# A norm turned by VectorE and DRAM instead of TensorE, in a two-layer decoder trunk

## The chip, the cores and the metric

The kernel runs on one core of one Trainium2 chip. The metric is the device time of one execution in microseconds; for the kernel before it is the median of three runs, 1269.65 us (1269.5 to 1270.11).

A core has a matrix engine (TensorE; PE in the profile, its weight loads PEld), VectorE (DVE), ScalarE (ACT) and GpSimd (POOL), and a fifth engine, SyncE (SP), that only issues transfers. Each engine works through its own queue in order. TensorE accumulates into banks of PSUM, from which VectorE and ScalarE read.

## What is computed

Two layers over 256 tokens of width 1024, all in float32. Cut to what matters here, one layer is

```python
h = layer_norm(ALPHA * x + 0.5 * swiglu(x, ffn1_w_gu, ffn1_w_down), ln_g[0], ln_b[0])
(dn_q, dn_k, dn_v, dn_b, dn_a, dn_z, sw_q, sw_k, sw_v, xa_q, gates) = split(h @ w_in)
o_dn = deltanet_branch(...)              # gated delta rule
o_sw = sliding_window_attention(...)     # banded attention
o_xa = memory_cross_attention(xa_q, mem_n, w_mem_kv)   # k, v = split(mem_n @ w_mem_kv)
merged = sum over branches of sigmoid(gates) * (branch @ w_branch)
h = layer_norm(ALPHA * h + merged @ w_out, ln_g[1], ln_b[1])
x = layer_norm(ALPHA * h + 0.5 * swiglu(h, ffn2_w_gu, ffn2_w_down), ln_g[2], ln_b[2])
```

The change concerns the first of the three norms of each layer, the one that stands ahead of the three mixers, and the matmuls that come next.

## The kernel before, in words

**Tiling.** The 256 tokens are two blocks of 128 rows (`tb` 0 and 1). A matmul contracts over 128 partitions, so the activations are also needed with features on partitions: `hT`, eight slices of 128 features by 256 tokens. The matmuls take operands of the format fp32r, so every operand is split into a high part (a rounded copy, made by ScalarE) and a low part (the rest, made by VectorE): `split`, line 125. Each product is three matmuls, high by high, high by low, low by high (`mm3`, line 139).

**Weights** come in one stream, in units of at most 128 x 1024 (`unit`, line 104). SyncE loads a unit into one of four `raw` buffers, ScalarE and VectorE split it into one of five `whi` and five `wlo` buffers. Units are scheduled ahead of other work, and each buffer comes free when TensorE has used it.

**Order.** The program is traced once, and a planner orders each engine's queue by priority and by its own model of times. The kernel bends this order in two ways. `tc.issue_after(x)` puts instructions behind `x` in the queue of `x`'s engine. `pinned` keeps TensorE's instructions in program order; it is on in the mixers.

**Around the norm.** The down projection of the feed-forward (`Ffn.rest`, line 375, which calls `projA`, line 181) ends with the last four units for the first block, then for the second. `Post` (line 395) adds the residual and normalises: `layernorm` (line 268) takes the statistics, then multiplies twice (lines 291 and 296), in two halves of 512 columns. After each half `fin(c)` calls `to_T` (line 249): four TensorE transposes of 128 x 128 through PSUM (line 137, tile `sm`), then a split from PSUM into `hT`. For the first block these calls are kept back as `turns`, and `projA` runs them between the last matmul groups of the second block; for the second block they are made at once.

**Behind the norm** come the memory projections (`memory_kv`, line 512), which don't need `hT`: keys with four units (96 matmuls of width 256), values with four units (48 of width 512). The low halves of the value units stand behind the norm's last instruction on VectorE (`behind=post.end`, `held`). The values are copied out of PSUM by ScalarE (line 521). Then the mixers begin with the first projection of `h`, 648 columns wide (line 529): eight units, each used for six matmuls of width 324 by each block. The last three units (`tail`) are kept and used block after block; the first five go unit by unit, both blocks each. The four PSUM banks of this projection are those that the memory keys and values held before.

**The DRAM trip** that the change uses is in the kernel already, in the feed-forward (`Ffn.out`, lines 353 to 363, and `settle`): VectorE's transpose turns each 32 x 32 block on its own (line 356), GpSimd issues four writes to a DRAM tile `tr` (line 362) and one read back as `pt` (line 363), which puts the 32 x 32 blocks where they belong. ScalarE and VectorE then split `pt`.

On GpSimd's queue two memsets (lines 849 and 850) prepare buffers for the delta rule's inverses.

Of the kernel before, what the change touches and what calls it, by code (L numbers as in the profile page):

```python
# [17 lines left out]
P = 128  # L18
D = 1024
S = 256  # L20
# [3 lines left out]
KD = D // P  # L24
# [4 lines left out]
MOD = 648  # L29
# [9 lines left out]
def tile_trunk(ctx, tc, x, xT, mem, memT_, wst, lnp, memln, cvw, rows, cst, out):  # L39
    nc = tc.nc  # L40
# [83 lines left out]
    def split(hi, lo, src):  # L124
        return nc.scalar.copy(hi, src).ins, nc.vector.tensor_tensor(lo, src, hi.bitcast(F32), op=ALU.subtract).ins  # L125
# [183 lines left out]
    class Ffn:  # L309
        def __init__(self, before=None):  # L310
            self.units = []
            for q in range(KD // 2):
                if before:
                    before(q)
                self.units.append(unit(cuts=2 if before and q == 0 else 1, parts=2 if before and q in (1, 2) else 1))
            self.hu, self.bank, self.due = {}, {}, []
# [77 lines left out]

    class Post:

        def __init__(self, g_ap, b_ap, last=False):
            self.aps, self.last, self.hT = (g_ap, b_ap), last, None

        def early(self, bank):  # L400

# [6 lines left out]
        def __call__(self, tb, outs):  # L408
            if tb == 0:
                self.gb = gb(*self.aps)  # L410
                self.hT = None if self.last else new_hT()
            y = hres[tb]

            def put(q):
                return self.hT[0][:, q * 4:q * 4 + 4, :], self.hT[1][:, q * 4:q * 4 + 4, :]

            def src(j, c):
                nc.vector.scalar_tensor_tensor(y[:, c], outs[tb][j], 0.5 / ALPHA, y[:, c], op0=ALU.mult, op1=ALU.add)

            turns = []  # L420

            def fin(c):
                if self.last:

                    cc = slice(c * 512, (c + 1) * 512) if not tb else slice(*((0, 512), (512, 768), (768, 1024))[c])
                    (nc.scalar if c == 2 else nc.sync).dma_start(out[tb * P:(tb + 1) * P, cc], y[:, cc])
                elif tb == 0:

                    turns.append(lambda: to_T(put, tb, y, c))
                else:  # L430
                    to_T(put, tb, y, c)

            self.end = layernorm(y, *self.gb, 1, src, fin, [o.shape[-1] for o in outs[tb]], (512, 256, 256) if self.last and tb else (512, 512))
            return turns

    def begin(nxt, hT):
# [72 lines left out]
            return {8: lambda: again(0), 12: lambda: once(0), 14: lambda: again(1), 18: lambda: once(1)}  # L509
        return {4: vecs, 6: lambda: sums(0), 8: rows_, 11: halves_, 12: lambda: quarter(0), 14: lambda: quarter(1), 16: lambda: quarter(2), 18: lambda: quarter(3)}  # L510

    def memory_kv(mT, behind):
        mx = (lambda k: mT[k // 4][:, k % 4, :], lambda k: mT[2 + k // 4][:, k % 4, :])
        mkT = (T(pu, [P, 4, S], "u10", F32R), T(pu, [P, 4, S], "u7", F32R))
        for i, b in enumerate(projB(mx, 4, 2)):
            split(*(t[:, 2 * i:2 * i + 2, :] for t in mkT), b)
        mv_ = T(pu, [P, 2, 512], "u11")
        outs = [[acc()] for _ in range(2)]
        projA(mx, 512, 2, KD, outs, behind=behind, held=range(4))
        for tb in range(2):  # L520
            nc.scalar.copy(mv_[:, tb, :], outs[tb][0])
        return mkT, mv_

    def mixers(l, hT, mkT, mv_, post):
        xt = acc_of(hT)
        pinned[0] = True

        outs = [[acc()[:, :MOD // 2] for _ in range(2)] for _ in range(2)]
        projA(xt, MOD, 1, KD, outs, 3)
        ba = T(pu, [P, 2, 8], "ba")  # L530
        zs = T(pu, [P, 2, 512], "u3")
        swv = T(pu, [P, 2, P], "swv")
# [288 lines left out]
        def inverses():  # L821

            cp = T(p2, [P, 2, 4, 16], "t2", bufs=4)
            for c in range(2):
                tmp = T(p2, [P, 4, P], "t2", bufs=4)
                nc.vector.tensor_tensor(tmp, AK[c][:, :, 0, :], over4(cs[:, C_NB:C_NB + P]), op=ALU.mult)
                nc.vector.tensor_reduce(cp[:, c], tmp.rearrange("p h (d i) -> p h i d", i=16), axis=AX.X, op=ALU.add)
            dr = T(pd, [P, P], "dr")
            nc.gpsimd.dma_start(dr, cp.rearrange("p c h i -> p (c h i)"))
            blocks = dr.rearrange("(d j) n -> d (j n)", j=16)  # L830
            for t in range(2):
                src = blocks[:, t * 1024:(t + 1) * 1024].unsqueeze(1).to_broadcast([8, 16, 1024])
                nc.gpsimd.dma_start(TM[t].rearrange("p a h c -> p (a h c)"), src)
            for c in range(2):
                for q in qd:
                    nc.gpsimd.tensor_tensor(L32[q, c], AK[c][q, :, 0, q], cs[q, C_LV:C_LV + 32].unsqueeze(1).to_broadcast([32, 4, 32]), op=ALU.mult)

            y16 = T(p2, [P, 8, 16], "t2", bufs=4)
            pr16 = T(p2, [P, 8, 15], "t2", bufs=4)
            i16 = cs[:, C_I16:C_I16 + 16].unsqueeze(1).to_broadcast([P, 8, 16])  # L840
            nc.gpsimd.tensor_copy(y16, i16)
            ab = [TM[c].rearrange("p a h (n i) -> p (a h) n i", i=16) for c in range(2)]
            for j in range(15):
                n = 15 - j
                nc.gpsimd.tensor_tensor(pr16[:, :, 0:n], ab[j // 8][:, j % 8, :, j + 1:16], y16[:, :, j:j + 1].to_broadcast([P, 8, n]), op=ALU.mult)
                nc.gpsimd.tensor_tensor(y16[:, :, j + 1:16], y16[:, :, j + 1:16], pr16[:, :, 0:n], op=ALU.add)
            nc.gpsimd.tensor_tensor(Y32.rearrange("p c h (d i) -> p (c h) d i", d=2), y16.unsqueeze(2).to_broadcast([P, 8, 2, 16]),
                                    cs[:, C_BD:C_BD + 32].rearrange("p (d i) -> p d i", d=2).unsqueeze(1).to_broadcast([P, 8, 2, 16]), op=ALU.mult)
            nc.gpsimd.memset(Y, 0.0)
            nc.gpsimd.memset(X64[qd[0], :, :, 32:64], 0.0)  # L850

        W = T(pu, [P, 1024], "w0")
        X64, X32, Y32 = (W[:, a:b].rearrange("p (c h i) -> p c h i", c=2, h=4) for a, b in ((0, 512), (512, 768), (768, 1024)))
# [277 lines left out]
    for l in range(NL):  # L1131
        mT = []
        mid = memory_T(mT, l)
        if l == 0:

            mid[2] = lambda: load(cs, cst)
            more = {4: lambda *a: xres(0), 6: lambda *a: xres(1), 8: lambda *a: small()}
        post = Post(lnp[l, 0, 0], lnp[l, 0, 1])
        f1.rest(hT, 4, [((pu, "u0"), (pu, "u1")), ((pu, "u2"), (pu, "u3"))], post, mid, ends, {} if l else more)
        kv = memory_kv(mT, post.end)  # L1140
        if l == 0:
            nc.scalar.activation(nea, rw[:, :, 8:12], AF.Exp)
            nc.vector.tensor_scalar(nea, nea, -1.0, None, ALU.mult)
        post2 = Post(lnp[l, 1, 0], lnp[l, 1, 1])
        mixers(l, post.hT, *kv, post2)
        f2 = Ffn()
        begin(f2, post2.hT)
        last = l == NL - 1
        post = Post(lnp[l, 2, 0], lnp[l, 2, 1], last)
        f2.rest(post2.hT, 6, [((pu, a), (pu, b)) for a, b in (("u0", "u1"), ("u2", "u3"), ("u4", "u5"), ("u6", "u13"))], post, behind=post2.end)  # L1150
        ends = post.end
        if not last:
            f1, hT = Ffn(), post.hT
            begin(f1, hT)
# [9 lines left out]
def _stream(i):  # L1164
    parts = []
    for l in range(NL):
        def ffn(gu, dn):
            for c in range(0, FF, S):
                parts.append(_kcols(np.concatenate([gu[:, c:c + S], gu[:, FF + c:FF + c + S]], 1), 2))

            parts.append(_kcols(dn.reshape(FF // S, 4, 2, 32, D).transpose(0, 2, 1, 3, 4).reshape(FF, D), 1))
        ffn(i["ffn1_w_gu"][l], i["ffn1_w_down"][l])
        mk = i["w_mem_kv"][l]
        parts.append(_kcols(mk[:, :512], 2))
        parts.append(_kcols(mk[:, 512:], 2))
        w = i["w_in"][l]
        parts.append(_kcols(np.concatenate([w[:, 1536:2056], w[:, 2696:2824]], 1), 1))
        for s in (512, 0, 1024, 2824):
            parts.extend(_kcols(w[:, c:c + 256], 4) for c in (s, s + 256))
        parts.append(_kcols(w[:, 2568:2696], 8))  # L1180
        sq = w[:, 2056:2568].reshape(D, 2, 4, 64).transpose(0, 2, 1, 3).reshape(D, 512)
        parts.extend(_kcols(sq[:, s:s + 256], 4) for s in (0, 256))
        wb = i["w_branch"][l]
        for n in (2, 1, 0):
            for j in range(2):
                c = 3336 + n * D + j * 512
                parts.append(_kcols(w[:, c:c + 512], 2))
            b = wb[n]
            if n == 1:
                b = b.reshape(2, 4, 64, D).transpose(1, 0, 2, 3).reshape(512, D)  # L1190
            parts.append(_kcols(b, 1))
        parts.append(_kcols(i["w_out"][l], 1))
        ffn(i["ffn2_w_gu"][l], i["ffn2_w_down"][l])
    return np.concatenate(parts)
# [47 lines left out]
```

## Time and profile before

| | before |
|---|---|
| median of three runs | 1269.65 us |
| profiled execution | 1269.55 us |
| its span | 1267.8 us |
| TensorE busy | 1257.0 us (99%) |
| VectorE busy | 870.5 us (69%) |
| ScalarE busy | 661.0 us (52%) |
| GpSimd busy | 221.7 us (17%) |
| granted TensorE clock | 0.999 |
| DRAM traffic | 263.56 MB, mean 208 GB/s |

The span is the time from the first to the last instruction of the program; the time of an execution has a little more around it. Lines such as L134 are lines of the kernel, and `acc<-whi,hT` names an output tile and its inputs. In a timeline, the columns are start and duration in us, engine, line, operation, tiles, shape and count; a bracket gives idle time before the first of them and what ended it. In the chain of waits, the columns are start, duration, and the piece of work. Matmuls overlap in the pipeline, so the cost of one is the distance between starts, not its duration.

### The profile page before, as it was taken

Reading aid. Unit: us, or ns where it says so; the run is one execution under the profiler, and the core shown is the slowest. Engines: PE = TensorE matmul, PEld = TensorE weight load, DVE = VectorE, ACT = ScalarE, POOL = GpSimd, SP = SyncE. Lnnn points to the kernel's source line nnn. Section 1 sums busy time; section 2 is a strip of 40 time slices with the busy share of each in tenths; the row PEclk is TensorE's granted clock in tenths of the full one; section 3 lists DMA queues with packets and bytes.
Section 4 is the critical chain, followed back from the end, with each engine's and each line's share of the span. In section 5 each row is a group of like instructions: output and inputs, shape, how many; then the busy total and the mean of one; then the engine's idle time right before and its main releaser. Section 6 shows DMA issues by size and latency. Waiting matters only on the chain.

```text
span 1267.8 us, 18770 instructions
## 1 busy us (share of the span) xinstructions
PE 1257.0 (99%) x6916; PEld 1070.2 (84%) x6916; DVE 870.5 (69%) x1284; ACT 661.0 (52%) x982; POOL 221.7 (17%) x395
## 2 busy tenths in 40 slices
PE   9999999999999999999999999999999999999997
PEld 6888889999878888888888888899988788888886
DVE  6678576886667776665666656759767588766565
ACT  6456544665664544454454554456656654454441
POOL 1232100002331102221012220000033401122100
PEclk9999999999999999999999999999999999999999
DMA  8988765665554738887668886566564456588862
GB/s 293 315 270 280 253 212 157 210 183 132 169 152 147 250 136 256 242 242 222 216 206 245 257 256 216 183 184 205 163 167 134 134 191 225 179 245 244 241 223 80
DMA packets 78795, 263.56 MB, mean 208 GB/s; under 512 B 12528, under 2 KB 13968, under 8 KB 78704
## 3 DMA queue, kind: packets, MB, share of 16 engines
q1 hardware_dynamic: 66320, 232.40, 57.2%
q0 software_dynamic: 12240, 29.84, 8.8%
q8 instruction: 54, 0.88, 0.3%
q14 instruction: 37, 0.30, 0.1%
q10 hardware_dynamic: 144, 0.13, 0.0%
HBM read 247.48 MB, written 14.85 MB: 207 GB/s over the span
## 4 chain that ended last, share of the span: by engine, by line
PE 99%; DMA 0%; DVE 0%; SPq 0%; ACT 0%; issue 0%; DVEq 0%
PE acc L134 87%; PE at L134 4%; PE sm L134 3%; PE sm L137 1%; PE acc L332 1%; PE acc L333 1%; PE acc L335 1%; PE at L137 1%; DMA raw<-in_wst_dram 0%; DVE h L291 0%; DVE h L296 0%; SPq L115 0%; SPq L78 0%; ACT whi L125 0%; DVE bnst L277 0%
## 5 line engine op out<-in xcount | busy, mean ns | idle before, releaser
L125 DVE TENSOR_TENSOR wlo<-raw,whi 128x1024 fp32r<-128x1024 f32 (+2 forms) x405 | 487.2, 1210 | 277.0 <-ACT whi L125 275.2
L125 ACT CAST whi<-raw 128x1024 fp32r<-128x1024 f32 (+2 forms) x405 | 413.5, 1029 | 397.4 <-PE acc L134 317.2
L134 PE MATMUL acc<-whi,hT 128*128 128x512 f32 (+1 forms) x1824 | 562.1, 386 | 0.8 <-ACT whi L125 0.8
L134 PEld LDWEIGHTS acc<-whi,hT 128*128 128x128 f32 x1824 | 340.0, 188 | 72.0 <-ACT whi L125 2.7
L134 PE MATMUL acc<-wlo,hT 128*128 128x512 f32 (+1 forms) x912 | 350.3, 384 | 0.0
L134 PE MATMUL acc<-whi,u 128*128 128x512 f32 x812 | 259.5, 392 | 0.0
L134 PEld LDWEIGHTS acc<-wlo,hT 128*128 128x128 f32 x912 | 171.3, 188 | 33.3 <-DVE wlo L125 1.3
L134 PEld LDWEIGHTS acc<-whi,u 128*128 128x128 f32 x812 | 152.3, 188 | 32.1 <-DVE u L125 0.5
L134 PE MATMUL acc<-wlo,u 128*128 128x512 f32 x406 | 158.2, 390 | 0.0
L362 POOL DMA_DIRECT2D tr<-t x176 | 96.3, 554 | 314.0 <-DVE t L356 307.4
L134 PE MATMUL acc<-hT,whi 128*128 128x256 f32 x672 | 121.8, 284 | 0.0
L134 PEld LDWEIGHTS acc<-hT,whi 128*128 128x128 f32 x672 | 104.7, 192 | 0.0
L134 PE MATMUL acc<-hT,wlo 128*128 128x256 f32 x336 | 95.1, 283 | 0.0
L134 PEld LDWEIGHTS acc<-wlo,u 128*128 128x128 f32 x406 | 76.3, 188 | 15.4
L134 PEld LDWEIGHTS acc<-hT,wlo 128*128 128x128 f32 x336 | 64.4, 192 | 0.0
L363 POOL DMA_DIRECT2D pt<-tr x44 | 25.1, 570 | 192.0 <-DMA tr<-t 146.7
L353 ACT ACTIVATE t<-acc 128x256 f32<-128x256 f32 x88 | 33.5, 381 | 37.6 <-PE acc L134 37.6
L134 PE MATMUL acc<-u,u 128*128 128x512 f32 x186 | 46.4, 394 | 0.0
L354 DVE TENSOR_TENSOR t<-t,acc 128x256 f32<-128x256 f32 x88 | 36.7, 417 | 8.1 <-ACT t L353 4.1
L134 PEld LDWEIGHTS acc<-u,u 128*128 128x128 f32 x186 | 34.6, 188 | 7.5
L125 DVE TENSOR_TENSOR u<-pt,u 128x512 fp32r<-128x512 f32 x44 | 28.9, 657 | 9.3 <-ACT u L125 9.3
L553 DVE SCALAR_TENSOR_TENSOR t<-acc,cw,t 128x255 f32<-128x255 f32 (+2 forms) x72 | 34.5, 479 | 1.1
(245 smaller groups left out, 1164.3 us busy)
## 6 DMA issues: line engine op xcount, KB each, us to landing
raw<-in_wst_dram SPq DMA_DIRECT2D x409, 512.0 KB, 4.3
tr<-t POOLq DMA_DIRECT2D x176, 64.0 KB, 3.7
pt<-tr POOLq DMA_DIRECT2D x44, 256.0 KB, 5.0
raw<-in_wst_dram SPq DMA_DIRECT2D x16, 324.0 KB, 3.0
gB<-in_lnp_dram SPq DMA_DIRECT2D x6, 512.0 KB, 5.9
bB<-in_lnp_dram SPq DMA_DIRECT2D x6, 512.0 KB, 6.2
w<-dr POOLq DMA_DIRECT2D x4, 512.0 KB, 10.4
t<-in_xT_dram SPq DMA_DIRECT2D x4, 256.0 KB, 5.6
```

The costliest lines, as they stand in the source:

```text
L125: return nc.scalar.copy(hi, src).ins, nc.vector.tensor_tensor(lo, src, hi.bitcast(F32), op=ALU.subtract).ins
L134: return pe(nc.tensor.matmul(*a, **k))
L137: return pe(nc.tensor.transpose(*a))
L332: nc.tensor.matmul(ps, hT[0][:, k, ts], hi[:, c], start=k == 0, stop=False)
L333: nc.tensor.matmul(ps, hT[0][:, k, ts], lo[:, c], start=False, stop=False)
L335: nc.tensor.matmul(ps, hT[1][:, k, ts], hi[:, c], start=False, stop=k == KD - 1)
L353: act = nc.scalar.activation(t[:, :, tb, :], g, AF.Silu).ins
L354: ins = nc.vector.tensor_tensor(t[:, :, tb, :], t[:, :, tb, :], u, op=ALU.mult).ins
L362: nc.gpsimd.dma_start(d[:, :, q].rearrange("b c x -> c b x"), z[32 * q:32 * q + 32].rearrange("c (b x) -> c b x", b=4))
L363: back = nc.gpsimd.dma_start(y, d.rearrange("b c q x -> (b c) (q x)")).ins
L553: nc.vector.scalar_tensor_tensor(yc[:, j, d:], b[:, j, :S - d], w[:, t:t + 1], yc[:, j, d:], op0=ALU.mult, op1=ALU.add)
```

## The change

For the norm ahead of the mixers alone (`bounce=True`), the transposes leave TensorE. As soon as a half of a block is normalised, VectorE transposes it in 32 x 32 blocks (`leave`). After the second half of a block GpSimd issues four writes of 128 KB to a DRAM tile `tn`. After the second block's last write it issues four reads of 256 KB, two for each block. Back in `pt`, features stand on partitions in another order than before, so the rows of `w_in` are reordered on the host to match. `land` splits what came back into `hT`.

Where the splits stand is written out by hand. The first block's come behind the splits of the memory keys on both engines. The second block's come behind the last copy of the memory values on ScalarE. The first projection takes its first four units for the first block alone, then the same four for the second (`lead=4`). `post.end`, behind which the low halves of the value units stand, is now the second block's last VectorE transpose. The two memsets stand behind the last read.

```diff
     class Post:
+        def leave(self, tb, y, c):
+            if not c:
+                self.z = T(p2, [P, D], "pp")
+            cc = slice(c * 512, (c + 1) * 512)
+            ins = nc.vector.transpose(self.z[:, cc], y[:, cc]).ins
+            if c:
+                d = T(pd, [4, 32, 4, S], "tn")
+                for q in range(4):
+                    out_ = nc.gpsimd.dma_start(d[:, :, q].rearrange("b c x -> c b x"), self.z[32 * q:32 * q + 32].rearrange("c (b x) -> c b x", b=4)).ins
+                self.backs[tb] = d
+            if tb and c:
+                with tc.issue_after(out_):
+                    for t, d in self.backs.items():
+                        back = self.backs[t] = T(p2, [P, 2, 512], "pt")
+                        for i in range(2):
+                            self.read = nc.gpsimd.dma_start(back[:, i].rearrange("p (q x) -> p q x", q=4), d[:, :, :, i * P:i * P + P].rearrange("b c q x -> (b c) q x")).ins
+            return ins
+
+        def land(self, tb, c):
+            ts = slice(tb * P, (tb + 1) * P)
+            hi, lo = (self.hT[n][:, c * 4:c * 4 + 4, ts].rearrange("p k (q s) -> p q k s", q=4) for n in range(2))
+            return split(hi, lo, self.backs[tb][:, c].rearrange("p (q k s) -> p q k s", q=4, k=4))
...
+                elif self.bounce:
+                    self.left = self.leave(tb, y, c)
                 elif tb == 0:
                     turns.append(lambda: to_T(put, tb, y, c))
...
+            if self.bounce:
+                self.end = self.left
             return turns
...
-    def memory_kv(mT, behind):
+    def memory_kv(mT, post):
+        behind = post.end
...
         for i, b in enumerate(projB(mx, 4, 2)):
-            split(*(t[:, 2 * i:2 * i + 2, :] for t in mkT), b)
+            ends = split(*(t[:, 2 * i:2 * i + 2, :] for t in mkT), b)
+        with tc.issue_after(ends[0]), tc.issue_after(ends[1]):
+            for c in range(2):
+                post.land(0, c)
...
         for tb in range(2):
-            nc.scalar.copy(mv_[:, tb, :], outs[tb][0])
+            copied = nc.scalar.copy(mv_[:, tb, :], outs[tb][0]).ins
+        with tc.issue_after(copied):
+            for c in range(2):
+                post.land(1, c)
...
-        projA(xt, MOD, 1, KD, outs, 3)
+        projA(xt, MOD, 1, KD, outs, 3, lead=4)
...
-            nc.gpsimd.memset(Y, 0.0)
-            nc.gpsimd.memset(X64[qd[0], :, :, 32:64], 0.0)
+            with tc.issue_after(post0.read):
+                nc.gpsimd.memset(Y, 0.0)
+                nc.gpsimd.memset(X64[qd[0], :, :, 32:64], 0.0)
...
-        post = Post(lnp[l, 0, 0], lnp[l, 0, 1])
+        post = Post(lnp[l, 0, 0], lnp[l, 0, 1], bounce=True)
...
-        w = i["w_in"][l]
+        w = i["w_in"][l].reshape(4, KD, 32, -1).transpose(1, 0, 2, 3).reshape(D, -1)
```

More of the change, by code (lines that the diff above doesn't have):

```diff
@@ L395, in tile_trunk, with __init__ @@
     class Post:
-        def __init__(self, g_ap, b_ap, last=False):
+        def __init__(self, g_ap, b_ap, last=False, bounce=False):
             self.aps, self.last, self.hT = (g_ap, b_ap), last, None
+            self.bounce, self.backs = bounce, {}
+        def leave(self, tb, y, c):
[19 more added lines that the diff above has]
+            return split(hi, lo, self.backs[tb][:, c].rearrange("p (q k s) -> p q k s", q=4, k=4))
         def early(self, bank):
@@ L520, in memory_kv, with mixers @@
         for tb in range(2):
-            nc.scalar.copy(mv_[:, tb, :], outs[tb][0])
+            copied = nc.scalar.copy(mv_[:, tb, :], outs[tb][0]).ins
+        with tc.issue_after(copied):
+            for c in range(2):
+                post.land(1, c)
         return mkT, mv_
-    def mixers(l, hT, mkT, mv_, post):
+    def mixers(l, hT, mkT, mv_, post0, post):
         xt = acc_of(hT)
@@ L1137, in tile_trunk @@
             more = {4: lambda *a: xres(0), 6: lambda *a: xres(1), 8: lambda *a: small()}
-        post = Post(lnp[l, 0, 0], lnp[l, 0, 1])
+        post = Post(lnp[l, 0, 0], lnp[l, 0, 1], bounce=True)
         f1.rest(hT, 4, [((pu, "u0"), (pu, "u1")), ((pu, "u2"), (pu, "u3"))], post, mid, ends, {} if l else more)
-        kv = memory_kv(mT, post.end)
+        kv = memory_kv(mT, post)
         if l == 0:
@@ L1144, in tile_trunk @@
         post2 = Post(lnp[l, 1, 0], lnp[l, 1, 1])
-        mixers(l, post.hT, *kv, post2)
+        mixers(l, post.hT, *kv, post, post2)
         f2 = Ffn()
```

## The prediction, made before the change was run

> **What bounds the kernel now.** I read the page first, then the chain of waits around the norm of layer 0, then the timelines of TensorE, ScalarE, VectorE and GpSimd there. The page gives busy time and the chain that ended last:
>
> ```profile
> PE 1257.0 (99%) x6916; PEld 1070.2 (84%) x6916; DVE 870.5 (69%) x1284; ACT 661.0 (52%) x982; POOL 221.7 (17%) x395
> PE 99%; DMA 0%; DVE 0%; SPq 0%; ACT 0%; issue 0%; DVEq 0%
> ```
>
> Both name TensorE, so time is won by taking instructions or gaps from TensorE, and lost by making it wait. The profiled execution took 1269.55 us for a span of 1267.8; the median of the three runs is 1269.65, so the sum below can be made against 1269.55.
>
> The chain of waits around the change in layer 0, and its summary over an equal stretch of layer 1 (811.2 to 853.2 us):
>
> ```profile
> 187.29 0.55 PE sm L137 x4
> 187.84 0.12 PE acc L134
> 187.96 0.54 PE sm L137 x4
> 188.50 6.40 PE acc L134 x54
> 194.90 0.59 PE sm L137 x4
> 195.49 0.12 PE acc L134
> 195.62 0.59 PE sm L137 x4
> 196.20 29.85 PE acc L134 x180
> ```
>
> ```profile
> by line: PE acc L134 88.4%; PE at L134 6.7%; PE sm L137 5.4%; issue 0.0%
> ```
>
> L137 is the transpose that the change removes, in four groups of four per layer; all else is matmul without a pause. From 54 matmuls in 6.40 us, one of width 256 takes 0.12 us.
>
> **What goes from TensorE.** In layer 0 the first two groups stand from 187.29 to 188.50 with one matmul of 0.12 inside: 1.21 - 0.12 = 1.09 us. The second two stand from 194.90 to 196.20, again with one: 1.30 - 0.12 = 1.18. Together 2.27 us. In layer 1 the line has 5.4% of 42 us, also 2.27. So 4.54 us go.
>
> A second, smaller piece is at the head of the first projection (width 324), in layers 0 and 1:
>
> ```profile
> 211.97 0.31 PE L134 MATMUL acc<-whi,hT 128*128 128x324 f32 x1
> ...
> 213.15 0.71 PE L134 MATMUL acc<-whi,hT 128*128 128x324 f32 x2
> 213.70 0.31 PE L134 MATMUL acc<-wlo,hT 128*128 128x324 f32 x1
> ```
>
> ```profile
> 840.38 0.71 PE L134 MATMUL acc<-whi,hT 128*128 128x324 f32 x2
> 840.94 0.30 PE L134 MATMUL acc<-wlo,hT 128*128 128x324 f32 x1
> ```
>
> From 211.97 to 213.15 eight matmuls start, 0.147 us apart. The two from 213.15 take until 213.70, so 0.55 instead of 0.29: TensorE stood 0.26 us. In layer 1 it is 840.94 - 840.38 = 0.56, again 0.26. The second of the two, the tenth matmul, is the first on the second bank of the second token block, and the last value copy frees that bank:
>
> ```profile
> 203.82 0.73 ACT L125 CAST whi<-raw 128x648 fp32r<-128x648 f32 x1 [1.69 <-issue]
> 206.62 0.73 ACT L125 CAST whi<-raw 128x648 fp32r<-128x648 f32 x1 [2.07 <-PE acc L134]
> 209.37 0.73 ACT L125 CAST whi<-raw 128x648 fp32r<-128x648 f32 x1 [2.02 <-PE acc L134]
> ...
> 212.81 0.58 ACT L521 COPY u<-acc 128x512 f32<-128x512 f32 x1
> ```
>
> The copy ends at 213.39. With four units of the first block in front, the second block starts 24 x 0.147 = 3.53 us after the projection does, and the copies stand before the second block's splits, so this wait should be gone: 2 x 0.26 = 0.52 us.
>
> **What is put in its place, and whether it is hidden.** The norm's rows now go VectorE transpose, four writes to DRAM for each block, two reads for each, then the splits. The prices come from the same trip in the first feed-forward block, in the order VectorE, GpSimd, ScalarE:
>
> ```profile
> 132.69 0.71 DVE L356 STREAM_TRANSPOSE t<-t 128x512 f32<-128x512 f32 x1
> 133.32 0.65 DVE L125 TENSOR_TENSOR u<-pt,u 128x512 fp32r<-128x512 f32 x1
> ```
>
> ```profile
> 133.69 2.20 POOL L362 DMA_DIRECT2D tr<-t  x4 [6.06 <-DVE t L356]
> 139.81 0.57 POOL L363 DMA_DIRECT2D pt<-tr  x1 [3.92 <-DMA tr<-t]
> ```
>
> ```profile
> 145.09 0.62 ACT L125 CAST u<-pt 128x512 fp32r<-128x512 f32 x1 [0.53 <-DMA pt<-tr]
> ```
>
> A transpose occupies VectorE for 0.63 us (133.32 - 132.69) and ends at 133.40; the first write is issued at 133.69, the read at 139.81, and ScalarE gets its data at 145.09. Trip: 145.09 - 133.40 = 11.69 us. When does it start? VectorE in layer 0:
>
> ```profile
> 189.59 1.27 DVE L125 TENSOR_TENSOR hT<-sm,hT 128x512 fp32r<-128x512 f32 x2
> 190.77 0.41 DVE L418 SCALAR_TENSOR_TENSOR h<-at,h 128x256 f32<-128x256 f32 x1
> ...
> 194.02 1.41 DVE L296 SCALAR_TENSOR_TENSOR h<-h,rstd,bB 128x512 f32<-128x512 f32 x2
> 195.35 3.49 DVE L125 TENSOR_TENSOR wlo<-raw,whi 128x1024 fp32r<-128x1024 f32 x3
> ...
> 204.58 0.83 DVE L125 TENSOR_TENSOR wlo<-raw,whi 128x648 fp32r<-128x648 f32 x1 [1.47 <-ACT whi L125]
> ```
>
> The first block's two transposes (1.26) take the room of the two splits at 189.59 (1.27), so the second block's last step starts at 194.02 as before. With a transpose behind each half the last one ends at 194.02 + 1.41 + 1.26 = 196.7. By the trip above the first half of the first block is there at 208.4, its high part is split at 209.0 and its low part (0.62 + 0.65) at 209.7. TensorE reaches the projection at 211.97 - 2.27 = 209.70, and needs the low part two matmuls later, at 210.0. So at the feed-forward's price it is just in time. Both ends of that price:
>
> ```profile
> DMA to landing us min/median/max: 2.0/3.7/5.6
> ```
>
> ```profile
> DMA to landing us min/median/max: 3.2/5.0/6.2
> ```
>
> The first is for the 64 KB writes (L362), the second for the 256 KB reads (L363). The last write is issued at 196.7 + 0.29 + 3 x 0.55 = 198.6; with about 0.6 us between landing and read (an estimate: the rest of 139.81 - 133.69 after three issues and the 3.7), data come between 198.6 + 2.0 + 0.6 + 3.2 = 204.4 and 198.6 + 5.6 + 0.6 + 6.2 = 211.0. The new writes carry 128 KB each and four reads follow one another, which speaks for late. The traffic of the two places speaks for early; its last two columns are the busy share of the DMA engines and GB/s:
>
> ```profile
> 126.00:154.00 28.00, 28.00 (x126) 23.17 (x125) 16.21 (x18) 14.09 (x17) 3.90 (x7) 1.00 0.82 272
> 187.00:212.00 25.00, 25.00 (x164) 22.34 (x163) 18.40 (x30) 12.09 (x17) 0.34 (x2) 1.00 0.40 115
> ```
>
> The memory projections leave the engines idle 60% of the time, the feed-forward 18%. I therefore take 207 to 208.4, and no wait. The Trainium skill ("DMA: Bandwidth & Descriptors", section "Anatomy of one DMA — SWDGE (gpsimd) path") has 2.0 us plus bytes over 436 GB/s for one such transfer: 2.3 us for a write, 2.6 for a read, data at 204.1 and again no wait. The rows here are slower than that rule (3.7 for 64 KB, where it gives 2.15), so the rows decide; by it the wait rival below would have almost no chance.
>
> The rest costs nothing, with these covers. The low halves of the memory value units stand behind the norm's last instruction, now 1.35 us later (196.7 for 195.35): the first is ready at 196.7 + 1.16 = 197.9. TensorE meets it here:
>
> ```profile
> 200.78 0.39 PE L134 MATMUL acc<-whi,w 128*128 128x512 f32 x1
> ```
>
> 200.78 - 2.27 + 0.23 = 198.7, so 0.8 us stay; if that cover went, each 0.1 us would cost 0.1. The second block's data come two read issues (1.1 us) later and are needed 3.53 us later. The first projection's fourth unit is cast at 209.37 and its low part takes 0.83 us behind that, ready by 211.0 - 2.27 = 208.7; with the first block alone in front it is needed at 209.7 + 18 x 0.147 = 212.3. The two memsets that now stand behind the reads on GpSimd's queue are wanted by the inverses only, tens of microseconds later, and SyncE's queue of weight loads is not touched.
>
> Sum: 1269.55 - 4.54 - 0.52 = **1264.5 us**.
>
> **The rivals.**
> *The trip is late and TensorE waits.* For it: the cover of 0.3 us at the feed-forward's price, and larger transfers. Against: the idle DMA engines. At the late end, 211.0, the low part is ready at 212.3 and TensorE waits 2.3 us in each layer: 1264.5 + 4.6 = 1269.1, no change.
>
> *The splits block ScalarE and VectorE (slower).* Both engines work in order. The first block's splits are only held behind the memory key splits; if they stand ahead of the casts of 203.82, 206.62 and 209.37, these wait for the DRAM trip. With data at time L, the second weight unit's low part is ready at L + 0.62 + 2 x 0.65 + 0.83 = L + 2.75, and TensorE wants it at 209.70 + 7 x 0.147 = 210.7. At 208.4 that is 0.4 us a layer; at 211.0 it is 3.0, which gives 1270.6. It turns slower by over 0.2% (past 1272.1) when a layer loses 3.8 us, at L = 211.8, past the late end. If doubled transfers push L to 212.5, the loss is 4.5 a layer: 1264.5 + 9.0 = 1273.5. A sentence of the Trainium skill speaks for such lateness: "VectorE: DVE Perf Modes", section "The three transpose paths", calls a plain DMA copy that transposes by strides 19 times slower than the crossbar's when the innermost stride is large. Here the runs are whole (1 KB written, 512 B read), and the feed-forward's trips, with runs of 512 B written, land in 5.6 us at worst, so I give it little.
>
> *The value units are late.* If VectorE's order puts more ahead of them than the two transposes, the 0.8 us cover goes; one more low half (1.16) would cost 0.4 us a layer, 1265.3, and two 1.5 a layer, 1267.5.
>
> **How the numbers follow.** About 0.2% (2.5 us) is what a measurement of this kernel can tell from no change: faster means under 1267.1, slower over 1272.1. Chances: hidden 0.64, trip late 0.22, value units late 0.08, splits blocking 0.06. A late trip of up to 1.3 us a layer is still faster; with a quarter of that rival (0.05) and 0.07 of the value case, faster has 0.76, slower the 0.06 of blocking, no change 0.18. The range goes from 1263.6 (a further microsecond where VectorE is relieved) to 1267.9, a wait of 1.7 us a layer; outside lie blocking and the late half of the first rival.
>
> **What would show it.** Right: no L137 on `sm<-cs,h` at these two norms, the projection's first matmul near 209.7 and 2 x 2.27 us earlier in layer 1, no stretch over 0.3 us in it, ScalarE getting the first block's data before 208.5. Wrong: idle time of TensorE in front of that matmul put down to the split of `hT`, a weight split of width 648 that waits behind a split of `hT`, or writes that land over 6 us after issue.

## The result and the profile after

The changed kernel takes 1265.24 us (median of six runs, 1264.12 to 1266.23), the kernel before 1269.58 beside it (1269.07 to 1270.11): a ratio of 0.9966 with a 95% interval of 0.9953 to 0.9979. That is 4.3 us or 0.34% less, for a forecast of 1264.5. The profiled execution took 1265.74 us for a span of 1263.8.

The page of after, busy times and chain:

```profile
PE 1252.4 (99%) x6884; PEld 1067.8 (84%) x6884; DVE 878.2 (69%) x1292; ACT 661.0 (52%) x982; POOL 235.4 (19%) x419
PE 98%; DMA 1%; DVE 0%; SPq 0%; issue 0%; ACT 0%; DVEq 0%
```

TensorE has 32 instructions fewer and 4.6 us less to do; VectorE has 7.7 us more, GpSimd 13.7 more. TensorE is the bound as before. The chain of waits of after, in layer 0:

```profile
187.96 42.10 PE acc L134 x284
```

and in layer 1:

```profile
813.05 41.98 PE acc L134 x283
```

Where four groups of transposes stood there is now one unbroken run of matmuls, through the memory projections and the first projection. Just ahead of it, in both kernels, stand 24 matmuls into a tile named `at`; their end is a common point to count from. From there to the first matmul of width 324 it was 211.97 - 187.29 = 24.68 us in layer 0 of before. TensorE's timeline of after has that matmul at 210.35, and in layer 1 at 835.44:

```profile
210.35 0.32 PE L134 MATMUL acc<-whi,hT 128*128 128x324 f32 x1
...
213.32 0.46 PE L134 MATMUL acc<-whi,hT 128*128 128x324 f32 x2
213.62 0.31 PE L134 MATMUL acc<-wlo,hT 128*128 128x324 f32 x1
```

```profile
835.44 0.32 PE L134 MATMUL acc<-whi,hT 128*128 128x324 f32 x1
```

210.35 - 187.96 = 22.39 and 835.44 - 813.05 = 22.39: 2.29 us less, for 2.27 forecast. In the projection's head 22 matmuls start between 210.35 and 213.62, 0.149 us each, so the stop at the tenth is gone too.

The trip itself in layer 0 of after, on VectorE, GpSimd and ScalarE:

```profile
195.80 1.30 DVE L406 STREAM_TRANSPOSE pp<-h 128x512 f32<-128x512 f32 x2
```

```profile
191.11 2.19 POOL L410 DMA_DIRECT2D tn<-pp  x4 [49.94 <-DVE pp L406]
197.40 2.17 POOL L410 DMA_DIRECT2D tn<-pp  x4 [4.10 <-DVE pp L406]
199.56 1.51 POOL L417 DMA_DIRECT2D pt<-tn  x2
204.27 1.49 POOL L417 DMA_DIRECT2D pt<-tn  x2 [3.21 <-ACT whi L125]
```

```profile
207.63 0.73 ACT L125 CAST whi<-raw 128x648 fp32r<-128x648 f32 x1 [1.21 <-DMA raw<-in_wst_dram]
208.27 1.14 ACT L125 CAST hT<-pt 128x512 fp32r<-128x512 f32 x2
```

and the landing of the first block's two reads (L417, from 199 to 202 us):

```profile
DMA to landing us min/median/max: 6.4/6.7/7.0
```

The first block's reads are issued right behind the last write, at 199.56 and 200.3, with no bracket, so they waited for nothing; its own writes were done. The first lands at 199.56 + 6.4 = 206.0, the second at 200.3 + 7.0 = 207.3. The second block's reads leave only at 204.27: they had to wait, and their own writes were issued at 197.40 and later. ScalarE takes the data at 208.27, also without a bracket: it came late because of the weight cast ahead of it, which had waited for its load. The first high part is ready at 208.27 + 0.57 = 208.84 and wanted at 210.35, which leaves 1.5 us of cover. In layer 1 ScalarE gets them at 832.96, with a wait for the read:

```profile
832.96 0.62 ACT L125 CAST hT<-pt 128x512 fp32r<-128x512 f32 x1 [2.14 <-DMA pt<-tn]
```

Ready at 833.58, wanted at 835.44: 1.9 us of cover.

### The profile page after: what moved, and what is told of

It reads as the page before. It is cut to its first block, busy times and chain, and to the rows that moved or that the text cites. A ratio compares the mean times of both kernels' runs of the same rounds, so it can differ in the third digit from the quotient of the medians.

```text
span 1263.8 us, 18750 instructions
## 1 busy us (share of the span) xinstructions
PE 1252.4 (99%) x6884; PEld 1067.8 (84%) x6884; DVE 878.2 (69%) x1292; ACT 661.0 (52%) x982; POOL 235.4 (19%) x419
## 4 chain that ended last, share of the span: by engine, by line
PE 98%; DMA 1%; DVE 0%; SPq 0%; issue 0%; ACT 0%; DVEq 0%
PE acc L134 87%; PE at L134 4%; PE sm L134 3%; PE sm L137 1%; PE acc L332 1%; PE acc L333 1%; PE acc L335 1%; PE at L137 1%; DMA raw<-in_wst_dram 1%; DVE h L291 0%; DVE h L296 0%; SPq L115 0%; SPq L78 0%; ACT whi L125 0%; DVE bnst L277 0%
```

## The experiments

My theory: the gain is TensorE's own work, the 32 transposes and the short stop, and the trip costs nothing because other matmuls run meanwhile. The rivals: the trip costs part of it back; the gain comes from the projection's new order and not from the transposes; the order of the splits matters little.

All times below are medians; the kernel before took 1269.58 to 1269.86 us beside them, 1269.23 beside the last.

| run | what it is | us (lowest to highest) | ratio to before, 95% interval |
|---|---|---|---|
| e1_lead0 | after without the lead | 1270.25 (1268.56 to 1273.48) | 1.0006, 0.9997 to 1.0015 |
| e2_lead_only | before with the lead | 1269.04 (1268.12 to 1270.13) | 0.9994, 0.9985 to 1.0003 |
| e3_pe_back | after, transposes put back | 1269.4 (1268.79 to 1270.7) | 0.9997, 0.9988 to 1.0006 |
| e4_no_trip | after without the DRAM trip | 1265.96 (1265.13 to 1266.66) | 0.9971, 0.9961 to 0.9982 |
| e5_hold3 | reads held back by 3 memsets | 1272.16 (1270.42 to 1273.13) | 1.0019, 1.0010 to 1.0028 |
| e6_hold6 | reads held back by 6 memsets | 1272.01 (1269.71 to 1274.84) | 1.0020, 1.0011 to 1.0029 |
| e7_lands_first | second splits ahead of value copies | 1266.94 (1265.63 to 1269.56) | 0.9982, 0.9973 to 0.9991 |
| r_after | after again, beside e5 to e7 | 1265.8 (1263.88 to 1268.32) | 0.9970, 0.9961 to 0.9979 |
| e8_mem_trip | a second trip, memory attention | 1272.66 (1270.57 to 1274.71) | 1.0023, 1.0014 to 1.0032 |
| r_after2 | after again, beside e8 | 1266.2 (1264.34 to 1267.02) | 0.9970, 0.9959 to 0.9982 |
| e9_mem_trip2 | e8 in another order | 1270.01 (1267.87 to 1274.9) | 1.0013, 1.0003 to 1.0023 |

**Is it the transposes? (e3_pe_back)** The kernel after, but TensorE makes its transposes as well, and nothing reads them:

```diff
                     self.left = self.leave(tb, y, c)
+                    again = lambda: [transpose(ps[:, j * P:(j + 1) * P], y[:, (c * 4 + j) * P:(c * 4 + j + 1) * P], ident) for ps in [sm()] for j in range(4)]
+                    if tb:
+                        again()
+                    else:
+                        turns.append(again)
```

> The changed kernel with the 32 TensorE transposes put back, their results unused. Main theory (they cost the room that they took, 2.3 us a layer): 4.6 us over the changed kernel, about 1269.8. Rival (part of the gain had other causes): clearly less than 4 us over it.

1269.4 us, before's time within what can be told apart. By the ratios to before that is 3.4 to 3.9 us over the two series of after, somewhat less than the 4.6 of the theory; with about 1.1 us of uncertainty on each ratio, the clock alone does not settle between theory and rival. The trace does. The chain of e3 in layer 0 has the groups back, 0.55 + 0.54 + 0.63 + 0.59 = 2.31 us:

```profile
187.21 0.55 PE sm L137 x4
...
187.88 0.54 PE sm L137 x4
...
194.62 0.63 PE sm L137 x4
...
195.36 0.59 PE sm L137 x4
```

With the trip and the new order in place and the transposes' time back, the gain is gone. It is the transposes; what is missing to 4.6 us is taken up below, under the sum.

**Does the trip cost anything? (e4_no_trip)** This kernel leaves out the writes and the reads, so its features are in a wrong order; the two memsets no longer stand behind the last read:

```diff
-                d = T(pd, [4, 32, 4, S], "tn")
...
-            if tb and c:
-                with tc.issue_after(out_):
...
+                self.backs[tb] = self.z.rearrange("p (c x) -> p c x", c=2)
```

> The changed kernel without the DRAM trip: the splits read what VectorE turned, so the features reach the projection in a wrong order. Main theory (the trip is hidden and its traffic costs nothing): the time of the changed kernel, within 0.5 us of 1265.2. Rival (its traffic delays weights and takes back part of the gain): 0.7 us or more under it, 1264.5 or less.

1265.96 us, the same as with the trip to what can be told apart (about 1 us). The windows of 187 to 212 us, of after and then of e4 (the last two columns are the DMA engines' busy share and GB/s):

```profile
187.00:212.00 25.00, 25.00 (x165) 22.80 (x164) 20.77 (x34) 12.43 (x18) 8.62 (x14) 1.00 0.67 199
```

```profile
187.00:212.00 25.00, 25.00 (x163) 22.80 (x163) 20.61 (x34) 13.32 (x19) 1.26 (x2) 1.00 0.43 128
```

TensorE is busy all 25 us in both. The trip takes 7.4 us of GpSimd and raises the DMA engines' share from 0.43 to 0.67, and none of it reaches the end.

**What is the lead for? (e1_lead0, e2_lead_only)** One word in each, taken from after and put into before:

```diff
-        projA(xt, MOD, 1, KD, outs, 3, lead=4)
+        projA(xt, MOD, 1, KD, outs, 3)
```

> The changed kernel, but the first projection takes both blocks unit by unit again. Main theory (the four leading units cover the second block's trip): the second block is needed 0.9 us after the projection starts, its splits are done about 1.5 us (layer 0) to 1.9 us (layer 1) later than that, so 3 to 4 us over the changed kernel, 1268.5 to 1269. Rival (the leading units only relieve the bank that the value copies hold): 0.5 us over it, 1265.7.

> The kernel before with the four leading units and nothing else. Main theory (they take away the 0.25 us wait for the bank in each layer): 0.5 us under the kernel before, 1269.1. Rival (the order alone is worth nothing, or costs because buffers come free later): 1269.6 or more.

Alone, the lead measures 0.7 us (1269.04; the interval goes from 1.9 us faster to 0.4 slower), in line with the 0.52 of the forecast but not to be told from nothing. Taken from after it costs 4.5 to 5 us (1270.25 for 1265.24 and 1265.8), more than either theory gave it, and the whole gain with it. TensorE's timeline of e1 in layer 1, with a matmul of the second block, and e1's windows there (the column ahead of the last two is the granted clock):

```profile
838.75 0.41 PE L134 MATMUL acc<-whi,hT 128*128 128x324 f32 x1 [1.95 <-ACT hT L125]
```

```profile
840.70:844.40 3.70, 3.70 (x17) 3.70 (x16) 1.29 (x2) 1.14 (x2) 0.00 (x0) 0.54 0.63 209
844.40:848.00 3.60, 3.60 (x26) 3.60 (x26) 1.21 (x2) 1.48 (x2) 0.00 (x0) 1.00 0.53 181
```

Without the lead the second block's data are wanted six matmuls (0.9 us) behind the first block's and not 24 (3.5 us). TensorE waits 1.95 us, and the matmuls after that run for 3.7 us at a granted clock of 0.54: 17 of them in 3.7 us, where the next window has 26 in 3.6. So this wait cost about 3.6 us, its own 1.95 and 3.7 x (1 - 0.54) = 1.7 of clock. In layer 0 the wait was 0.94 us and the clock stayed. With a second, short wait of 0.16 in each layer that makes 4.9 us, for 4.5 to 5 measured. The trip is only a part of the reason. In layer 1 the second block's first half lands at 831.89 + 6.0 = 837.9 and ScalarE splits it from 838.07 on; but in layer 0 it lands at 202.88 + 4.8 = 207.7, and ScalarE gets to it at 210.59, because a weight cast and the last value copy stand ahead of it. The lead makes room for the second block's landing and for ScalarE's queue; it is what makes the trip free, not a second gain beside it.

**How much cover is there? (e5_hold3, e6_hold6)** Memsets on GpSimd's queue between the last write and the first read, three in e5 and six in e6:

```diff
+                    backs = [T(p2, [P, 2, 512], "pt") for _ in range(2)]
+                    for n in range(3):
+                        hold = nc.gpsimd.memset(backs[n % 2].rearrange("p c x -> p (c x)"), 0.0).ins
+                with tc.issue_after(hold):
                     for t, d in self.backs.items():
```

> The changed kernel with three memsets of 1 us each on GpSimd ahead of the reads, so that what comes back is about 2.9 us late. Main theory (a cover of about half a microsecond before the first use in layer 1 and one to two in layer 0): layer 0 stays as it is, layer 1 waits about 1 us, 1 to 2 us over the changed kernel. Rival (the trip has several microseconds to spare): the time of the changed kernel.

> The same with six memsets, 5.8 us late. Main theory (the wait passes 2 us in each layer, and the granted clock then goes to half for some 3.4 us, as after the 1.95 us wait in the run with no leading units): waits of 2 to 3 us a layer and 1.7 us a layer for the clock, 7 to 10 us over the changed kernel. Rival (a wait costs only its own length): 4 to 6 us over it.

Both take about 1272.1 us, 6.3 more than r_after: e5 costs far more than I expected, and e6 lies between its two theories. That they are equal is chance, for they lose the time in different ways. GpSimd's timeline of e5 and of e6 in layer 0:

```profile
198.37 2.77 POOL L416 MEMSET pt<- 128x1024 f32 x3
203.08 2.99 POOL L421 DMA_DIRECT2D pt<-tn  x4 [1.94 <-DMA tn<-pp]
```

```profile
198.03 5.46 POOL L416 MEMSET pt<- 128x1024 f32 x6
203.42 3.00 POOL L421 DMA_DIRECT2D pt<-tn  x4
```

The runs are shifted against each other, so count from the start of the second block's writes (197.40 in after, 196.20 in e5, 195.86 in e6): the first read leaves after 2.2 us in after, 6.9 in e5 and 7.6 in e6, so 4.7 and 5.4 us late. In layer 1 it is 4.0 and 5.4.

In e5 the planner also changed the order of the reads. In the program as built, the first read in the queue is of the second block, and it waits for that block's writes (1.94 us); the first block's two stand behind it. In layer 1 the first block's first half lands at 831.87 + 6.4 = 838.3, counted as above 5.2 us later than in after. ScalarE waits for it, and TensorE for ScalarE:

```profile
838.32 1.24 ACT L125 CAST hT<-pt 128x512 fp32r<-128x512 f32 x2 [3.38 <-DMA pt<-tn]
```

```profile
838.99 0.42 PE L134 MATMUL acc<-whi,hT 128*128 128x324 f32 x1 [3.27 <-ACT hT L125]
```

5.2 us less the cover of 1.9 us is 3.3, and TensorE waited 3.27. In layer 0 the same half lands 3.8 us later than in after, and TensorE loses only 0.16. That fits as well: in after the half lay there for 2.3 us (206.0 to 208.27) before ScalarE took it, and with the 1.5 us of cover that makes 3.8.

In e6 the reads stand as in after. The first one lands at 203.42 + 4.3 = 207.7 in layer 0 (the first line below), and TensorE would have come to it at about 208.8. But ScalarE's queue is in another order than in after: a weight cast that waits for TensorE and a value copy now stand ahead of the split, so the data are taken 2.4 us after they landed, and TensorE waits:

```profile
DMA to landing us min/median/max: 4.3/4.3/4.3
```

```profile
209.02 0.73 ACT L125 CAST whi<-raw 128x648 fp32r<-128x648 f32 x1 [0.81 <-PE acc L134]
209.66 0.58 ACT L558 COPY u<-acc 128x512 f32<-128x512 f32 x1
210.13 1.14 ACT L125 CAST hT<-pt 128x512 fp32r<-128x512 f32 x2
```

```profile
210.81 0.42 PE L134 MATMUL acc<-whi,hT 128*128 128x324 f32 x1 [1.82 <-ACT hT L125]
```

In layer 1 the same cast and copy stand ahead, the split starts at 840.04, and TensorE again waits 1.82 us: the cast waits for TensorE's last value matmul, so everything behind it keeps the same distance. There the data land at 835.71 + 3.9 = 839.6, so most of that wait would be there with any order; in layer 0 all of it comes from the order. So e5 measures the cover, and e6 shows something that I had not asked for: a split that stood behind the wrong instruction cost as much as a late trip.

The sum for e6 is 2 x 1.82, 2 x 0.17 of a second short wait, and 1.7 for a stretch at half clock behind the first of the two: 5.7 of the 6.2 us. For e5 it is 3.27, 2 x 0.16 and again 1.7 (granted clock 0.50 from 840.1 to 843.5): 5.3 of the 6.4.

**Does the order of the splits matter? (e7_lands_first)** The second block's splits stand ahead of the value copies:

```diff
-        for tb in range(2):
-            copied = nc.scalar.copy(mv_[:, tb, :], outs[tb][0]).ins
-        with tc.issue_after(copied):
-            for c in range(2):
-                post.land(1, c)
+        for c in range(2):
+            landed = post.land(1, c)[0]
+        with tc.issue_after(landed):
+            for tb in range(2):
+                nc.scalar.copy(mv_[:, tb, :], outs[tb][0])
```

> The changed kernel with the second block's splits ahead of the value copies. Main theory (with four leading units the copies' bank is wanted 3.5 us after the projection starts, so their order is worth nothing while the data are there in time): the time of the changed kernel, within 0.5 us. Rival (the order is needed: the copies wait for the second block's data, the bank comes free late): 1 us or more over it.

1266.94 us, 1.1 more than r_after beside it; the two intervals overlap a little (0.9973 to 0.9979). The timeline of e7 shows the rival's wait, in layer 1 only: a bank is freed late by a value copy that stood behind a split which waited for the trip.

```profile
838.19 0.62 ACT L125 CAST hT<-pt 128x512 fp32r<-128x512 f32 x1 [1.03 <-DMA pt<-tn]
838.72 0.58 ACT L557 COPY u<-acc 128x512 f32<-128x512 f32 x1
```

```profile
840.47 0.42 PE L134 MATMUL acc<-whi,hT 128*128 128x324 f32 x1 [0.40 <-ACT u L557]
```

TensorE loses 0.6 us at that matmul (it starts 0.71 behind the one before it, not 0.15) and 0.4 at another three matmuls earlier, 0.9 in all, which agrees with the clock. The order that the change wrote out by hand is right, and worth about a microsecond.

**The same again (r_after, r_after2).**

> The changed kernel again. Main theory (its own gain is 5.1 us, and the first weight loads and the second norm of layer 0 move it by up to 1 us from run to run): 4 to 5 us under the kernel before, and in its profile the stretch from the norm to the first projection again 22.67 us in each layer.

> The kernel after once more, beside e8 on the same chip: 1265.2 to 1265.9, by both theories.

1265.8 and 1266.2: after stands at 1265.2 to 1266.2 in three series, 3.7 to 4.3 us ahead of the kernel before in each. Both repeats miss what I had put down, by 0.2 and 0.3 us. The stretch from the end of the `at` group to the projection is 22.39 or 22.40 us in both layers of both, as in after; the 22.67 above is not its length.

**Does the trip carry over? (e8_mem_trip, e9_mem_trip2)** The memory attention has transposes too, 16 in a layer:

```profile
303.07 0.87 PE at L137 x8
...
306.70 1.78 PE at L134 x16
```

These are eight transposes of the first block's probabilities in the chain of after, and the value products that use them. In e8 they become a trip:

```diff
+            zv = z.rearrange("p (b k h i) -> p k h b i", b=4, k=2, h=4)
+            for kb in range(2):
+                nc.vector.transpose(zv[:, kb], pr[:, :, kb * P:(kb + 1) * P].rearrange("p h (b i) -> p h b i", b=4))
...
         def x_turn(tb):
...
-                for h in range(4):
-                    transpose(ps[:, h, :], prs[tb][:, h, kb * P:(kb + 1) * P], ident)
-                (nc.vector.tensor_copy if kb else nc.scalar.copy)(pT[:, kb], ps)
+            for i in range(2):
+                nc.gpsimd.dma_start(back[:, 2 * i:2 * i + 2], d[:, :, 2 * i:2 * i + 2].rearrange("b c q x -> (b c) q x"))
```

> The kernel after, with the same trip applied to a second set of TensorE transposes: the probabilities of the memory attention (8 transposes for each block, 0.87 us a block in the chain of waits of after). VectorE turns them as soon as ScalarE has scaled them, four writes and two reads on GpSimd's queue bring them back, the copies out of PSUM go too, and the second block's value products stand two weave steps later, so that the trip has cover. Main theory (independent TensorE work as long as the trip is all that is needed): 2 x 2 x 0.87 = 3.5 us less than after, 1261.8 to 1262.8. Rival (the extra steps on VectorE and GpSimd, or the strided operand of the value products, cost TensorE as much as the transposes did): 1265 to 1268.

1272.66 us, 6.5 more than r_after2 and outside what either theory gave. TensorE's list of waits in e8 has two kinds that after does not have:

```profile
PE at L134 <- DMA pt<-tn: 6.4, 2, 3.5
PE at L134 <- DVE pp L821: 1.6, 1, 1.6
```

GpSimd's timeline of e8 shows the first: eight small products stood between the first block's two reads.

```profile
296.57 0.56 POOL L791 DMA_DIRECT2D pt<-tn  x1 [2.11 <-DMA tn<-pt]
297.15 5.75 POOL L878 TENSOR_TENSOR l<-u,cs 32x128 f32<-32x128 f32 x8
...
303.50 0.59 POOL L791 DMA_DIRECT2D pt<-tn  x1 [0.24 <-issue]
```

The second is a PSUM bank that the window scores held. e9 was to take both away by order alone:

```diff
+                    with tc.issue_after(x_read[0]):
...
-            7: [lambda: w_scores(0, 0)],
-            8: [lambda: w_scores(0, 1), lambda: x_values(1)]})
+            5: [lambda: w_scores(0, 0)],
+            6: [lambda: w_scores(0, 1)]})
         weave(branch(0, oX), {
+            1: [lambda: x_values(1)],
```

> e8 with its three waits taken away by order alone. The second read of the first block stands ahead of the eight GpSimd products (5.75 us) that it stood behind, so it lands by about 301 where it is needed at 304. The second block's value products move behind the first quarter of the next projection (near 324), since its reads landed at 319.9 and 322.8 in e8. The window scores move two steps forward, so that those products find a free bank. What stays is that a group of value products with its strided operand took 2.02 us in e8 for 1.78 in after, 0.24 a block, against 0.87 for the transposes. Main theory (e8 lost to waits alone): 4 x (0.87 - 0.24) = 2.5 us less than after, 1263.0 to 1264.0. Rival (the trip's traffic and the engines' other work delay something else by as much): 1265.5 or more.

1270.01 us, in the rival's range: by the ratios to before 1.3 us better than e8 and 5.5 behind after, by the medians 2.0 better and 4.4 behind. The first block's trip is free now. The second block's is not: the landing of its reads (L791, from 300 to 320 us), the window behind the wait, and the wait, all of e9:

```profile
DMA to landing us min/median/max: 9.4/10.0/10.7
```

```profile
324.10:327.50 3.40, 3.40 (x17) 3.40 (x18) 0.00 (x0) 0.00 (x0) 2.77 (x9) 0.58 0.49 194
```

```profile
324.08 3.41 PE L134 MATMUL at<-pt,u 128*128 128x128 f32 x16 [2.87 <-DMA pt<-tn]
```

The DMA engines are full there (share 1.03 from 308 to 320 us), and a read of the same 256 KB takes 9.4 to 10.7 us, not 5.1 to 7.0. They were full before this trip came: after has a share of 0.96 in the same 12 us. Beside the trip's reads in GpSimd's queue stand the two reads that spread the delta rule's blocks over all partitions; that these fill the engines is likely from their place, but it was not tried apart from the rest. The wait of 2.87 us brings half clock, so that the value products take 3.41 us for the 1.95 of the first block's. Against that stand the 0.87 us of the transposes. Placing these reads ahead of the spreading ones was not tried. The 0.24 us that I had put down for the strided operand is not there: the timelines give such a group 1.95 us in e9 and 1.95 in after, and the 2.02 of e8 is a piece of the chain that follows a wait.

## Why the prediction held, step by step

**The transposes.** Forecast 2.27 us a layer, measured 2.29 in the trace, and e3, which only puts the transposes back, loses the gain again. Shown.

**The stop in the projection.** Forecast 0.26 us a layer; it is gone from the timeline of after. By the clock alone it can't be told from nothing: e2, with only this, is 0.7 us faster with an interval across 1.

**The trip.** Forecast: data for ScalarE between 204.4 and 211.0, taken as 207 to 208.4, and no wait. ScalarE took them at 208.27, and e4 shows that the trip costs nothing that can be measured. But the number came out by luck, by two errors that offset each other. The prediction let the first block's reads wait for the second block's last write to land, with 0.6 us between landing and read (its own rows leave 139.81 - 133.69 - 3 x 0.55 - 3.7 = 0.8). In fact the first block's reads needed only their own block's writes, which had been issued from 191.11 on, and left at 199.56, right behind the last write. And a read was to take 3.2 to 6.2 us; these took 6.4 to 7.0, over the late end. A third step was wrong too: the second block's data were to come 1.1 us behind the first's, but its reads leave 4.7 us behind (204.27 for 199.56), and 4.5 in layer 1. The landing of all eight reads of after:

```profile
DMA to landing us min/median/max: 5.1/5.8/7.0
```

The writes, at twice the size, cost what the feed-forward's cost (median 3.8 for 3.7). The idle DMA engines, on which I counted, were not that idle with the trip on them (0.67 for 0.40). By the fit in the Trainium skill ("DMA: Bandwidth & Descriptors", section "Anatomy of one DMA — SWDGE (gpsimd) path") such a write and read would take an estimated 2.3 and 2.6 us; the trace does not agree (3.8 and 5.8), less still where the engines are full (9.4 to 10.7 in e9).

**The cover.** The 0.3 us of cover at the feed-forward's price became 1.5 and 1.9 us for the first block, and e5 confirms the 1.9 from outside (3.3 us of wait worked out from it, 3.27 measured). The second block has less, though the prediction gave it more. In layer 1 of after its low half is ready at 838.5 and wanted by the 27th matmul, at about 839.3; in r_after2 it is ready at about 839.0, and TensorE, whose last matmul started at 838.60, goes on only at 839.03:

```profile
839.03 0.56 PE L134 MATMUL acc<-whi,hT 128*128 128x324 f32 x2
```

That is 0.28 us lost, in one of the three profiles of after. So the trip came out free with almost nothing to spare, and the rival that it is late missed by a microsecond or two. One reason that layer 1 is tighter is that its last two writes stand 2.37 us behind the first two, put down to `issue`, in after, its repeats and e1, e3, e5, e6 and e7, but not in e8 and e9; why is not known.

**The other covers.** The value units' low halves and the two memsets cost nothing in after: the chain of after has no wait of TensorE in either stretch. The rival of blocked splits came in part, and cost nothing. In both layers the splits of `hT` stand behind the casts of three units, and the fourth unit's cast stands behind them. In layer 1, where the splits at 832.96 and 834.18 wait for their reads, that cast (width 648) waits with them, which the prediction named as a sign against it:

```profile
834.70 0.73 ACT L125 CAST whi<-raw 128x648 fp32r<-128x648 f32 x1
```

With the lead, the fourth unit is used 18 matmuls behind the first, at 835.44 + 18 x 0.149 = 838.1, and the cast ends at 835.43. e7 shows the same mechanism with a price, about 1 us, when the order is turned, and e6 its mirror: splits that stand behind casts.

**The sum.** 5.06 us forecast; on TensorE, 2.29 in each layer and the two stops make 5.1. The profiled execution shows 3.81 and the medians 4.3. Most of the rest of the profiled difference stands at two places. The first is the start of the kernel. There a matmul that waits for a weight cast starts at 10.26 us in after (a wait of 1.14) and at 9.65 in before (0.56): 0.6 us are lost before any changed instruction runs. r_after2 has no wait at that place, so this differs from run to run. The second is in front of the second norm of layer 0 in after:

```profile
453.99 1.33 PE L137 MATMUL sm<-cs,h 128*128 128x128 f32 x8 [0.37 <-issue]
```

Here not all of the gain is handed on. TensorE is 1.85 us earlier than in before (its `at` group starts at 444.16 for 446.01), but VectorE is only 0.6 earlier (line 296 of before starts at 445.82, the same step of after at 445.20). From 435.59 on VectorE works in after without a pause up to the norm's last step at 453.13. It started so late because low halves of weights stand ahead of the norm, and the cast that the first of them needs waited for a load in after (the second line) and not in before (the first):

```profile
435.10 1.03 ACT L125 CAST whi<-raw 128x1024 fp32r<-128x1024 f32 x1
```

```profile
434.50 1.05 ACT L125 CAST whi<-raw 128x1024 fp32r<-128x1024 f32 x1 [1.16 <-DMA raw<-in_wst_dram]
```

r_after, r_after2 and e4 have the same wait for a load, of 1.6 to 2.2 us, and TensorE waits 0.6 to 1.2 us at these transposes in them (in r_after another 1.0 in layer 1); before and e2 have neither wait. So a part of the gain that is missing goes, by the traces, to a weight stream that did not come as much earlier as TensorE did. No run tries this apart, and why the loads come late is open.

## What to carry to other kernels

A transpose on the engine that bounds the kernel can be moved to an idle engine and a trip through memory for its full price, here 2.29 us a layer, if matmuls that don't need it run for as long as the trip takes (here 13 us from VectorE's last step to TensorE's first use), and if the consumer takes first what comes back first: without the lead all of it was lost. Work out the cover from the traffic of that very place and from the in-order queues: the one in which the reads are issued, and the one in which the engine stands that takes the data (in layer 0 of e1 and e6 TensorE waited for data that had landed). The same trip elsewhere, with 12 to 16 us of other matmuls as cover, lost about 4.5 to 6.5 us where the DMA engines were full or GpSimd's products stood between the reads.

## What was not expected of the hardware

A wait of TensorE can cost nearly twice its length. Behind waits of 1.82 (layer 0 of e6), 1.95 (e1), 2.87 (e9) and 3.27 us (e5) the granted clock was 0.50 to 0.58 for about 3.4 us, which is some 1.7 us more; behind 0.94 us (e1), behind another wait of 1.82 us (layer 1 of e6) and even behind 2.82 us (layer 0 of e8) it stayed at 1.00. The windows of e6 behind its two equal waits:

```profile
212.20:215.60 3.40, 3.40 (x15) 3.40 (x14) 1.28 (x2) 0.62 (x1) 0.00 (x0) 0.50 0.41 159
```

```profile
842.20:845.60 3.40, 3.40 (x25) 3.40 (x24) 1.76 (x3) 1.24 (x2) 0.00 (x0) 1.00 0.53 189
```

The Trainium skill ("TensorE: Matmul & The Clock Gate", section "Part 1: The HAM clock gate (the "warmup" mystery)") describes a clock that falls to half rate after an idle window of about 3.4 us, counted by a window that runs freely. The length of the slow stretch and that equal waits fare differently agree with that; that 1.8 us of waiting is enough does not.
